# One pool of three PSUM banks for the prompt phase's row maxima, compressed outputs and transposes, in place of a pool of two and a pool of one

## The chip, the cores and the metric

The kernel runs on one core of a Trainium2 chip. The metric is the device time of one execution in microseconds (us). The core has a matrix engine (TensorE, PE in the profile, whose weight loads are listed as PEld), a vector engine (VectorE, DVE), a scalar engine (ScalarE, ACT), GpSimd (POOL) and SyncE (SP), which issues the transfers. Matrix results go to PSUM, which here is handed out as eight banks of 128 partitions by 512 fp32 values.

## The reference, cut to what matters

One decoder layer serves a prompt of 2048 tokens and a sample group of 32 tokens. Its attention branch, for 8 heads in 2 groups g of 4 heads r, looks at the keys in three ways and sums them with gates:

```python
sc = einsum('bgrtd,bngd->bgrtn', qg, kc) + bias        # compressed keys, 127 of them
pc = masked_softmax(sc, ...);  o_cmp = pc @ vc;  imp = pc @ cover
idx = top_k(score(imp), 8)                             # 8 blocks of 64 keys, per query
ps = masked_softmax(q @ k_selected + bias)             # selected branch "s"
pw = masked_softmax(q @ k_window + bias)               # window of 512 keys, branch "w"
o = g0 * o_cmp + g1 * (ps @ v_selected) + g2 * (pw @ v_window)
```

The rest of the layer is one input projection, a gated linear recurrence, two branch projections with gates, an output projection, a residual and a norm.

## The kernel before, in words

**Phases.** Up to about 1430 us of the span the kernel does the input projections beside the compression, the sample group's attention and the recurrence. Then comes the prompt phase (`prompt_phase`, line 1406), which the change touches. It walks 16 blocks of 128 queries in the order `ORDER` = 3, 2, 1, 0, 5, 4, 7, 6, ... , 12, 13 (line 1404); block number i stands for query tile t = ORDER[i].

**What a block needs.** Two blocks ahead, `prep` (line 1541) computes for each group g the compressed branch in five steps: `cmax` (the row maxima of the compressed scores, line 1550, reduced by DVE at 1552), `neg_row` (line 1416: two small DVE operations make `xd`, four PE products turn it into a row in PSUM, and ACT writes the row into the query operand, line 1426), `cs` (the scores, 1558 and 1559, and two exponentials on ACT), `cpv` (the compressed output, 12 products, read by a dozen small DVE operations that end in the choice of blocks `repp`, line 1579) and `sel` (a PE transpose, line 1584, and DVE writing the selection into the query operand, line 1585). One block ahead, `max_ops` (line 1488) computes row maxima of both branches: per chunk of up to 512 keys and head, products into a bank (lines 1518 and 1520) and one DVE reduction (line 1521); at the end `neg_row` again, whose row every final score product of that block (line 1643) needs. In the block itself, `score`, `probs` and `pv` make scores, exponentials and outputs, and `finish` (line 1656) transposes the block's sum (line 1660) and lets DVE multiply it (line 1672).

**Banks.** Eight are in use: two for `ps` (projections and, later, the merging products), two for `st` (scores), one for `po` (outputs), two in pool `pmx` (`mx`: every chunk of row maxima, `cmax`, `cpv`) and one in pool `ptr` (`tr`: `neg_row`, `sel`, `finish`). The code opens 608 tiles of `mx` and 128 of `tr` in the prompt phase. A tile is given a bank when its first product is scheduled, and the bank is free again after its last reader.

**Order of the work.** The order of each engine's queue is laid down when the kernel is built: the framework takes the instructions in program order, keeps a simulated time, and gives an engine the earliest instruction whose inputs and bank are ready by then. On the chip each engine goes through its queue in that order. Program order is made by hand in `run_block` (line 1883): list A holds the maxima of block i+1 and their `neg_row`, list B the `prep` steps of block i+2, both spread over the block's steps; `late` (line 1935) puts `finish` three steps behind its last output; `fill` (line 1850) puts in merging work (lines 1754 and 1786) of blocks that are done. Before the loop (lines 1607 to 1622) stand the `prep` of blocks 0 and 1 and the maxima of block 0. While the merging weights are not yet there, `fill` instead loads and splits them (`weights`, lines 1701 on ACT and 1702 on DVE), which in program order lies behind all that.

Of the kernel before, what the change touches and what calls it, by code (L numbers as in the profile page):

```python
# [10 lines left out]
F32 = mybir.dt.float32  # L11
# [7 lines left out]
PSUM = bass.MemoryType.PSUM  # L19
# [109 lines left out]
def trunk_kernel(ctx: ExitStack, tc: tile.TileContext, A, O):  # L129
# [1276 lines left out]
    def prompt_phase(a, st, pfill, state, sw):  # L1406
        KA, KB, V, TB, TQ = a["KA"], a["KB"], a["V"], a["TB"], a["TQ"]
        pu = st.enter_context(tc.tile_pool(name="pu", bufs=2, side="right"))
        pst = st.enter_context(tc.tile_pool(name="pst", bufs=2, space=PSUM, side="right"))
        ptr = st.enter_context(tc.tile_pool(name="ptr", bufs=1, space=PSUM, side="right"))  # L1410
        pmx = st.enter_context(tc.tile_pool(name="pmx", bufs=2, space=PSUM, side="right"))

        def flat(x):
            return x.rearrange("p r t -> p (r t)")

        def neg_row(m, dst):

            n = m.shape[2]
            x = pu.tile([128, 4, 4], F16, name="xd")[:, :, :2 * n]
            ve.tensor_scalar(x[:, :, :n], m, -1.0 / 1024, None, op0=OP.mult)  # L1420
            ve.scalar_tensor_tensor(x[:, :, n:], m, -1.0 / 1024, x[:, :, :n], op0=OP.mult, op1=OP.subtract)
            pt = ptr.tile([128, 4, 128], F32, name="tr")
            for r in range(4):
                mm(pt[:2 * n, r], x[:, r], a["id"], r == 0, True)

            ac.activation(dst, pt[:2 * n], AF.Identity, bias=a["nb"][:2 * n, n - 1:n], scale=1.0 / QS)

        def probs(ps, n, pool, bufs, sub):
            P = pool.tile([128, 512], F32, name="P", bufs=bufs[0])
            ph = pool.tile([128, 512], F16, name="Ph", bufs=bufs[1])  # L1430
            pl = pool.tile([128, 512], F16, name="Pl", bufs=bufs[1])
            ac.activation(P[:n], ps, AF.Exp, scale=1.0 / QS)  # L1432
            ac.activation(ph[:n], ps, AF.Exp, scale=1.0 / QS)  # L1433
            sub.tensor_sub(pl[:n], P[:n], ph[:n])  # L1434
            return ph, pl

        def pv(po, ph, pl, v, n, w, first, last):
            rs = [slice(r * 128, (r + 1) * 128) for r in range(4)]
            for r in range(4):
                mm(po[:, r, :w], ph[:n, rs[r]], v[:n, :w], first and r == 0, False)  # L1440
                mm(po[:, r, :64], ph[:n, rs[r]], v[:n, w:w + 64], False, False)  # L1441
            for r in range(4):
                mm(po[:, r, :w], pl[:n, rs[r]], v[:n, :w], False, last)  # L1443
# [44 lines left out]
        def max_ops(u, br, t, g):  # L1488
# [34 lines left out]
            def last():  # L1523
                ve.tensor_reduce(u["m"][:, :, "sw".index(br)], mp_[:, :, :nch], axis=AX.X, op=OP.max)
                if br == "s":
                    neg_row(u["m"], u["s"][96:100])
# [4 lines left out]
        def add_part(u, po, w):  # L1531

            new = "acc" not in u
            dst = pu.tile([128, 4, 64], F32, name="oacc", bufs=6) if new else pu.tile([128, 4, 64], F32, name="otmp", bufs=1)
            ve.tensor_tensor(dst, po[:, :, :64], w[:, :, None].to_broadcast([128, 4, 64]), op=OP.mult)  # L1535
            if new:
                u["acc"] = dst
            else:
                gp.tensor_add(u["acc"], u["acc"], dst)

        def prep(u, t, g):

            nv = 8 * t + 8
            nk = min(nv, 127)
            X = {}

            def cmax():
                pm = pmx.tile([128, 4, 128], F32, name="mx")
                for r in range(4):
                    mm(pm[:, r, :nv], u["c"][:96, r], u["k"][:96, :nv], r == 0, True)  # L1550
                m = pu.tile([128, 4], F32, name="mc")
                ve.tensor_reduce(m, pm[:, :, :nv], axis=AX.X, op=OP.max)
                ve.tensor_scalar(m, m, -10000.0 * QS, None, op0=OP.max)
                X["m"] = m

            def cs():
                ps = pst.tile([128, 512], F32, name="st")
                mm(ps[:nv], KB["c", g][:, :nv], flat(u["b"]), True, False)
                mm(ps[:nv], u["k"][:, :nv], flat(u["c"]), False, True)
                X["p"] = probs(ps[:nk], nk, pu, (1, 1), gp)  # L1560

            def cpv():
                po = pmx.tile([128, 4, 128], F32, name="mx")
                pv(po, *X["p"], V["c"][:, g], nk, 97, True, True)
                rs = po[:, :, 96]
                ve.tensor_scalar(rs, rs, TINY, None, op0=OP.max)
                ve.reciprocal(rs, rs)
                w = pu.tile([128, 4], F32, name="wc")
                ve.tensor_tensor(w, rs, gates[:, t, g * 4:g * 4 + 4], op=OP.mult)
                im = pu.tile([128, 32], F32, name="im")  # L1570

                for r in range(4):
                    ve.scalar_tensor_tensor(im, po[:, r, 64:96], rs[:, r:r + 1], im if r else a["sel0"][:, t], op0=OP.mult, op1=OP.add)
                add_part(u, po, w)
                m8 = pu.tile([128, 8], F32, name="m8p")
                ve.max(m8, im)
                rep = pu.tile([128, 32], F32, name="repp")
                ve.match_replace(rep, m8, im, -3e38)
                ve.tensor_tensor(rep, rep, im, op=OP.is_equal)
                X["rep"] = rep  # L1580

            def sel():
                pt = ptr.tile([128, 4, 128], F32, name="tr")
                pe.transpose(pt[:32, 0], X["rep"], ident)
                ve.tensor_scalar(u["s"][64:96], pt[:32, 0:1].to_broadcast([32, 4, 128]), -2.0 ** 15, None, op0=OP.mult)

            return [cmax, lambda: neg_row(X["m"][:, :, None], u["c"][96:98]), cs, cpv, sel]

        W_BUF = []
# [11 lines left out]
        def open_block(i):  # L1601
            units[i] = [loads(ORDER[i], g, i % 2) for g in range(2)]

        state["env"]["tp"] = lambda: ptr.tile([128, 4, 128], F32, name="tr").rearrange("p a b -> p (a b)")
        wc = sw.enter_context(tc.tile_pool(name="wc", bufs=3))
        state["env"]["piece"] = lambda: wc.tile([128, 512], F32, name="piece")
        for i in range(2):
# [16 lines left out]
        def main():  # L1624
# [29 lines left out]
            LA = {}  # L1654

            def finish(u, t, g, sz):
                pt = ptr.tile([128, 4, 128], F32, name="tr")
                ov = u["acc"].rearrange("p (a r) d -> p a (r d)", a=2)
                for k in range(2):
                    pe.transpose(pt[:, k], ov[:, k], ident)  # L1660
                q0 = t * 128
                rows = slice(g * 256, (g + 1) * 256)
                o = pp.tile([128, 2, 128], F32, name="oo", bufs=1)
                if t == ORDER[-1]:
                    if not LA:
                        for k in "hl":
                            LA["a" + k] = pu.tile([128, 512], F16, name="P" + k, bufs=1).rearrange("p (k t) -> p k t", k=4)
                    oh, ol = [LA["a" + k][:, 2 * g:2 * g + 2] for k in "hl"]
                else:
                    oh = pp.tile([128, 2, 128], F16, name="ooh", bufs=1)  # L1670
                    ol = pp.tile([128, 2, 128], F16, name="ool", bufs=1)
                ve.tensor_mul(o, pt[:, :2], sz)
                ac.activation(oh, o, AF.Copy)
                gp.tensor_sub(ol, o, oh)
                if t == ORDER[-1]:
                    return
                sy.dma_start(oah_d[rows, q0:q0 + 128].rearrange("(a p) t -> p a t", p=128), oh)
                sy.dma_start(oal_d[rows, q0:q0 + 128].rearrange("(a p) t -> p a t", p=128), ol)
# [204 lines left out]
            def run_block(i, t):  # L1883
# [24 lines left out]
                for x, (g, br, kt) in enumerate(tiles):  # L1908
# [14 lines left out]
                    if kt == t:  # L1923
                        epilogue(us[g], br, t, g, po)
                        if br == "s":
                            sz = pp.tile([128, 2, 128], F32, name="szt")
                            sy.dma_start(sz, sz_d[g * 256:(g + 1) * 256, t * 128:t * 128 + 128].rearrange("(a p) t -> p a t", p=128))

                            def fin(g=g, sz=sz):
                                finish(us[g], t, g, sz)  # L1930
                                if g == 1:
                                    done.add(t)
                                    fs["hold"] = max(fs["hold"], R["now"] + 4)

                            late.append((R["now"] + 3, fin))
# [22 lines left out]
    with ExitStack() as s2:  # L1958
        sw, sb = ExitStack(), ExitStack()
        load_x, fill, state = make_projections(s2, sw, sb)  # L1960
# [57 lines left out]
```

## Time and profile before

| what | value |
|---|---|
| median of 3 runs | 2497.49 us (2493.37 to 2504.09) |
| profiled execution | 2498.46 us, span of the core 2496.1 us |
| mean granted TensorE clock | 0.974 of full |
| PE busy | 2357.9 us (94% of the span) |
| DVE, ACT, POOL busy | 1575.8, 1198.0, 989.9 us |

The span is the time from the first to the last instruction of the core; the execution's own time has some 2 us around it. Busy times of different engines overlap, and an idle engine costs time only where others wait for it. A line "PE mx L1518 <- DVE mpw L1521" among the waits says that PE, at the product of line 1518 that writes a tile `mx`, sat idle until the DVE instruction of line 1521 that writes `mpw` was done: since that one reads the bank that PE wants to write, it is a wait for a bank.

### The profile page before, as it was taken

The page shows a single profiled execution, that of the slowest core. Times are in us where ns is not written, and L with a number is a line of the kernel's source. Part 1 is how long each engine was busy: PE and PEld are TensorE (multiplying, and loading weights), DVE is VectorE, ACT ScalarE, POOL GpSimd, SP SyncE. Part 2 cuts the span into 40 slices and gives each one's busy share as a digit, 9 for nine tenths or more (in the row PEclk, how much of TensorE's full clock was granted, in tenths as well). Part 3 has the DMA queues.
Part 4 walks back from the last instruction along what each step waited for, and adds up shares of the span by engine and source line. Part 5 has one row for each costly group of instructions (what it writes and reads, how often), then busy time and mean ns, then how long its engine had stood idle before and what let it go on. Part 6 is the DMA issues. An engine that isn't in the chain of part 4 may idle for free.

```text
span 2496.1 us, 57172 instructions
## 1 busy us (share of the span) xinstructions
PE 2357.9 (94%) x22228; PEld 1554.0 (62%) x22228; DVE 1575.8 (63%) x4232; ACT 1198.0 (48%) x2639; POOL 989.9 (40%) x1179
## 2 busy tenths in 40 slices
PE   5999999998999999999989969899999999999998
PEld 4988675554785555555555446656666666565765
DVE  7556455656325688777763667677777767767543
ACT  5544333422223366555552346436555666667763
POOL 0100102332102255444550006536656666677864
PEclk9999999999999999999999979999999999999999
DMA  6543314656322434333323652322222221211121
GB/s 202 170 121 115 121 69 163 218 205 217 131 65 105 144 105 132 115 118 97 109 87 98 192 159 63 79 81 69 78 58 72 57 66 51 63 52 45 48 59 46
DMA packets 266719, 264.96 MB, mean 106 GB/s; under 512 B 95100, under 2 KB 237872, under 8 KB 259280
## 3 DMA queue, kind: packets, MB, share of 16 engines
q1 hardware_dynamic: 257936, 223.56, 29.0%
q0 software_dynamic: 8512, 37.75, 4.6%
q8 instruction: 175, 2.87, 0.5%
q14 instruction: 96, 0.79, 0.1%
HBM read 181.84 MB, written 83.55 MB: 106 GB/s over the span
## 4 chain that ended last, share of the span: by engine, by line
PE 68%; DVE 14%; DMA 7%; ACT 4%; issue 4%; POOL 1%; SPq 1%; DVEq 0%; ACTq 0%; POOLq 0%
PE ps L361 14%; PE ps L440 9%; PE ps L1786 7%; PE ps L1754 6%; PE ps L421 4%; PE st L1643 3%; PE st L1633 3%; PE mx L1518 3%; DVE X L683 2%; DMA wraw<-in_w_in_dram 2%; PE ph L920 2%; PE po L1440 2%; PE po L1443 2%; PE po L1441 2%; DVE mps L1521 1%
## 5 line engine op out<-in xcount | busy, mean ns | idle before, releaser
L1434 POOL TENSOR_TENSOR Pl<-P,Ph 128x512 f16<-128x512 f32 (+5 forms) x444 | 516.6, 1173 | 406.8 <-ACT Ph L1433 171.6
L1432 ACT ACTIVATE P<-st 128x512 f32<-128x512 f32 (+3 forms) x444 | 264.6, 596 | 204.8 <-PE st L1643 157.5
L361 PEld LDWEIGHTS <-wh 128*128 128x128 f16 x2240 | 214.3, 99 | 190.4 <-issue 45.2
L1433 ACT ACTIVATE Ph<-st 128x512 f16<-128x512 f32 (+5 forms) x444 | 262.6, 593 | 14.9 <-PE po L1441 10.8
L361 PE MATMUL ps<-xh,wh 128*128 128x512 f16 (+1 forms) x1120 | 234.5, 344 | 11.0 <-DVE row L374 5.1
L1521 DVE TENSOR_REDUCE mps<-mx 128x1 f32<-128x512 f32 (+3 forms) x320 | 189.2, 605 | 75.9 <-PE mx L1518 45.7
L361 PE MATMUL ps<-xl,wh 128*128 128x512 f16 (+1 forms) x1120 | 236.0, 347 | 1.1 <-issue 1.0
L361 PE MATMUL ps<-xh,wl 128*128 128x512 f16 (+1 forms) x1120 | 232.3, 341 | 0.0
L440 PE MATMUL ps<-wh,xh 128*128 128x256 f16 (+3 forms) x680 | 189.4, 279 | 7.0 <-ACT to L447 4.3
L440 PE MATMUL ps<-wh,xl 128*128 128x256 f16 (+3 forms) x680 | 188.4, 278 | 4.0 <-DVE xl L327 4.0
L440 PE MATMUL ps<-wl,xh 128*128 128x256 f16 (+3 forms) x680 | 189.0, 278 | 0.0
L1440 PEld LDWEIGHTS <-Ph 128*128 128x128 f16 (+5 forms) x1776 | 138.8, 98 | 41.3 <-issue 6.9
L361 PEld LDWEIGHTS <-wl 128*128 128x128 f16 x1120 | 107.9, 98 | 86.3 <-issue 9.4
L1441 PEld LDWEIGHTS <-Ph 128*128 128x128 f16 (+5 forms) x1776 | 128.7, 96 | 32.7 <-issue 1.4
L440 PEld LDWEIGHTS <-xh 128*128 128x128 f16 (+1 forms) x1360 | 129.9, 99 | 30.7 <-issue 6.5
L686 POOL TENSOR_TENSOR X<-X,kt 128x128 f32<-128x128 f32 x160 | 81.8, 512 | 142.8 <-ACT X L685 142.8
L1521 DVE TENSOR_REDUCE mpw<-mx 128x1 f32<-128x512 f32 (+3 forms) x224 | 104.9, 485 | 49.6 <-PE mx L1520 46.7
L652 POOL TENSOR_TENSOR Xo<-Xo,qt 128x256 f32<-128x256 f32 x32 | 30.5, 953 | 260.4 <-ACT Xo L651 229.3
L1754 PEld LDWEIGHTS <-xh 128*128 128x128 f16 x1280 | 105.3, 98 | 30.3 <-issue 9.1
L1518 PE MATMUL mx<-kas,qs 96*128 96x512 f16 (+3 forms) x320 | 109.8, 355 | 10.4 <-DVE mps L1521 7.7
L1443 PEld LDWEIGHTS <-Pl 128*128 128x128 f16 (+3 forms) x1776 | 96.1, 97 | 30.9 <-POOL Pl L1434 8.4
L1440 PE MATMUL po<-vs,Ph 128*128 128x65 f16 x1088 | 106.6, 192 | 0.8 <-DVE otmp L1535 0.8
(538 smaller groups left out, 5918.9 us busy)
## 6 DMA issues: line engine op xcount, KB each, us to landing
wraw<-in_w_in_dram SPq DMA_DIRECT2D x22, 1024.0 KB
xt<-in_x_prompt_dram SPq DMA_DIRECT2D x32, 512.0 KB
ma_d<-row SPq DMA_DIRECT2D x8, 1040.0 KB
out_y_prompt_dram<-xt SPq DMA_DIRECT2D x16, 512.0 KB
sg<-ma_d SPq DMA_DIRECT2D x56, 128.0 KB
sg<-mb_d SPq DMA_DIRECT2D x56, 128.0 KB
mb_d<-row SPq DMA_DIRECT2D x18, 256.0 KB
q_d<-row SPq DMA_DIRECT2D x4, 1040.0 KB
```

Source lines behind the costliest of these rows:

```text
L361: mm(ps, l[:, kc], xs(r, t0, n)[:, kc], k == 0, k == 23)
L440: mm(ps, xs(l, t0, r)[:, kc], w[:, kc], k == 0, k == 23)
L1432: ac.activation(P[:n], ps, AF.Exp, scale=1.0 / QS)
L1433: ac.activation(ph[:n], ps, AF.Exp, scale=1.0 / QS)
L1434: sub.tensor_sub(pl[:n], P[:n], ph[:n])
L1440: mm(po[:, r, :w], ph[:n, rs[r]], v[:n, :w], first and r == 0, False)
L1441: mm(po[:, r, :64], ph[:n, rs[r]], v[:n, w:w + 64], False, False)
L1443: mm(po[:, r, :w], pl[:n, rs[r]], v[:n, :w], False, last)
L1518: mm(pmf[:, (x - ka) * 128:(y - ka) * 128], qq[:K, r], kk, i == 0, not sp_)
L1521: ve.tensor_reduce(mp_[:, r, c:c + 1], pmf[:, :n], axis=AX.X, op=OP.max)
L1754: mm(X["ps"], w[:, kc, cs], os_[o][:, kc], k == 0, k == 11)
L1786: mm(X["ps"], X["y"][y][:, kc, i0:i0 + r], W["o", kc // 4][w][:, kc % 4, cs], k == 0, k == 23)
```

## The change

The pool `ptr` is gone, `pmx` has three banks in place of two, and the tiles that were `tr` are taken from it under the name `mx`. All 736 tiles of the prompt phase now come from one pool. The number of banks in use stays eight. The last use that the diff touches (`env["tp"]`, for scaling projection weights) has no instruction left in the prompt phase: the last such load was at 1347.8 us.

```diff
-        ptr = st.enter_context(tc.tile_pool(name="ptr", bufs=1, space=PSUM, side="right"))
-        pmx = st.enter_context(tc.tile_pool(name="pmx", bufs=2, space=PSUM, side="right"))
+        pmx = st.enter_context(tc.tile_pool(name="pmx", bufs=3, space=PSUM, side="right"))
...
         def neg_row(m, dst):
-            pt = ptr.tile([128, 4, 128], F32, name="tr")
+            pt = pmx.tile([128, 4, 128], F32, name="mx")
...
             def sel():
-                pt = ptr.tile([128, 4, 128], F32, name="tr")
+                pt = pmx.tile([128, 4, 128], F32, name="mx")
...
-        state["env"]["tp"] = lambda: ptr.tile([128, 4, 128], F32, name="tr").rearrange("p a b -> p (a b)")
+        state["env"]["tp"] = lambda: pmx.tile([128, 4, 128], F32, name="mx").rearrange("p a b -> p (a b)")
...
             def finish(u, t, g, sz):
-                pt = ptr.tile([128, 4, 128], F32, name="tr")
+                pt = pmx.tile([128, 4, 128], F32, name="mx")
```

## Rows read from the trace of the kernel before

**Rows 1.** The page: busy times, and two of its 40-slice lines.

```profile
PE 2357.9 (94%) x22228; PEld 1554.0 (62%) x22228; DVE 1575.8 (63%) x4232; ACT 1198.0 (48%) x2639; POOL 989.9 (40%) x1179
...
PE   5999999998999999999989969899999999999998
...
PEclk9999999999999999999999979999999999999999
```

**Rows 2.** Windows: length; busy of PE, PEld, DVE, ACT, POOL; PEclk, DMA, GB/s.

```profile
1460.00:1503.00 43.00, 21.86 (x172) 12.66 (x171) 34.79 (x83) 18.94 (x27) 2.79 (x4) 0.53 0.53 157
...
1540.00:1600.00 60.00, 51.91 (x583) 33.08 (x582) 38.03 (x166) 32.76 (x63) 37.55 (x38) 1.00 0.25 63
1600.00:2400.00 800.00, 782.21 (x8646) 522.65 (x8645) 560.07 (x1498) 472.04 (x919) 509.63 (x493) 0.98 0.22 62
2400.00:2496.10 96.10, 84.89 (x1048) 57.31 (x1045) 38.04 (x121) 46.18 (x100) 51.99 (x57) 0.97 0.18 56
```

**Rows 3.** PE's waits from 1455 to 1503 us: total, times, longest.

```profile
PE mx L1518 <- DVE mpw L1521: 6.8, 5, 1.8
PE tr L1424 <- DVE qs L1585: 3.7, 1, 3.7
...
PE mx L1518 <- DVE mps L1521: 2.6, 2, 2.4
...
PE tr L1424 <- ACT qc L1426: 0.8, 1, 0.8
```

**Rows 4.** PE in order of time, 1450 to 1505 us: start, length, instruction.

```profile
1450.74 0.21 PE L1440 MATMUL mx<-vc,Ph 32*128 32x97 f16 x1
...
1452.58 0.25 PE L1550 MATMUL mx<-kac,qc 96*128 96x24 f16 x4
...
1459.89 0.27 PE L1584 MATMUL tr<-ident,repp 128*32 128x128 f32 x1 [0.78 <-DVE mc L1553]
...
1464.57 0.58 PE L1424 MATMUL tr<-h_id,xd 128*2 128x128 f16 x4 [3.72 <-DVE qs L1585]
...
1471.52 0.26 PE L1440 MATMUL mx<-vc,Ph 24*128 24x97 f16 x1 [0.61 <-ACT Ph L1433]
...
1474.81 0.61 PE L1518 MATMUL mx<-kw,qs 96*128 96x256 f16 x2 [1.52 <-DVE oacc L1535]
...
1488.65 0.42 PE L1584 MATMUL tr<-ident,repp 128*32 128x128 f32 x1
...
1502.17 1.01 PE L1643 MATMUL st<-qs,kw 100*128 100x512 f16 x2
```

**Rows 5.** DVE in order of time, 1460 to 1465 us.

```profile
1460.09 0.17 DVE L1421 SCALAR_TENSOR_TENSOR xd<-mc,xd 128x4 f16<-128x4 f32 x1
1461.11 2.70 DVE L1702 SCALAR_TENSOR_TENSOR xl<-wraw,swb,xh 128x1024 f16<-128x1024 f32 x2 [0.85 <-ACT xh L1701]
```

**Rows 6.** DVE's groups from 1460 to 1503 us: busy, mean ns, idle before.

```profile
L1702 DVE SCALAR_TENSOR_TENSOR xl<-wraw,swo,xh 128x1024 f16<-128x1024 f32 x8 | 10.3, 1282 | 3.8 <-ACT xh L1701 3.8
L1521 DVE TENSOR_REDUCE mps<-mx 128x1 f32<-128x512 f32 x8 | 5.4, 689 | 1.2 <-PE mx L1520 1.0
```

**Rows 7.** PE's waits from 1503 to 2400 us: total, times, longest.

```profile
PE mx L1518 <- DVE mps L1521: 5.8, 16, 1.0
...
PE mx L1518 <- DVE mpw L1521: 1.9, 5, 0.7
```

**Rows 8.** PE in order of time, between two blocks and near the end.

```profile
2021.54 0.59 PE L1550 MATMUL mx<-kac,qc 96*128 96x128 f16 x4
...
2026.64 0.58 PE L1424 MATMUL tr<-h_id,xd 128*4 128x128 f16 x4
...
2368.34 0.38 PE L1660 MATMUL tr<-ident,oacc 128*128 128x128 f32 x2
...
2370.12 0.38 PE L1518 MATMUL mx<-kas,qs 96*128 96x512 f16 x1
```

**Rows 9.** The window around that passage between two blocks, columns as in rows 2.

```profile
2015.00:2030.00 15.00, 12.43 (x98) 7.93 (x97) 13.17 (x31) 4.08 (x8) 4.24 (x4) 0.66 0.26 83
```

## The prediction

> **What bounds the kernel now.** I read the page first: PE is busy for 94% of the span, and nearly every slice of its line says 9 [rows 1]. So what any change of banks can give back is time in which PE idles or runs slowly. The clock line has one dip, just where the prompt phase begins. Windows over that phase [rows 2] then show where PE's time is lost: from 1460 to 1503 us PE is busy for 21.9 of 43 us, at a granted clock of 0.53, so mostly at the lower of its two levels (1.2 instead of 2.4 GHz); from 1540 to 1600 us it idles for 8.1 us; in the 800 us after that for 17.8 us in all. The last 96 us hold no maxima and are out of the change's reach. What PE waits for there is the third view. In the first stretch [rows 3] the largest wait is for a bank of maxima (6.8 us for branch "w", 2.6 us for "s", together 9.4), and next the single bank of transposes (3.7 and 0.8 us). In the 897 us from 1503 on, the waits for banks of maxima are small: 5.8 and 1.9 us [rows 7], 7.7 in all.
>
> One property of the pools has to be read from the order of time. If the 736 tiles are numbered in program order and set against the starts in the trace, no `mx` tile starts before an earlier `mx` tile, and no `tr` tile before an earlier `tr` tile. Across the two pools 180 tiles do start before an earlier one of the other pool. The first is the `cmax` of block 1 at 1452.58 us, which program order has behind the `sel` of block 0 that runs at 1459.89 [rows 4]; the last is a `finish` at 2368.34 us, which stands behind the maximum that starts at 2370.12 [rows 8]. So a pool hands out its banks in program order, and after the change these 180 can no longer overtake.
>
> **The change, part by part.** No instruction is added or removed: the same products, reductions and transposes run, no DMA moves to another place in the program, and no engine is given other work. What changes is which bank a product waits for, and with that the order in which the queues are laid.
>
> *The single transpose bank at the start.* The `neg_row` of block 1 has its `xd` complete by 1460.26 us (1460.09 + 0.17) [rows 5], but its products start at 1464.57, after 3.72 us of waiting for DVE line 1585 [rows 4]. That one empties the transpose bank; DVE spent 2.70 us on two weight splits in between [rows 5]. The second `neg_row` waits another 0.8 us for the first one's reader [rows 3]. With three banks neither waits: 4.5 us. They lie on a chain, since behind them stand the compressed scores, the compressed outputs of block 1 (the second at 1471.52 us) and only then the first row maximum, at 1474.81 [rows 4]. So the outputs come at about 1467.0.
>
> *The order of one pool at the start.* Against this, the maxima of block 0 now stand behind the `sel` of block 1, of which the second runs at 1488.65 us today, 13.8 us behind the first maximum [rows 4]. How long it takes when nothing overtakes it the trace doesn't show. The nearest rows are those of block 0, where the second compressed output starts at 1450.74 and the second `sel` at 1459.89: 9.15 us. From 1467.0 that gives 1476.2, so the maxima start 1.4 us later than now. Bounds: 4.5 us earlier if the `sel` is no hindrance, some 13.8 later if its place stays. I take +1.4, since the rows of block 0 are the same instructions.
>
> *The third bank for the maxima of block 0.* From 1474.81 us 16 maxima pass, 8 reductions for each branch, at 0.69 us [rows 6] 11.0 us of DVE; PE waited 9.4 us for their banks [rows 3]. In those gaps DVE took weight splits of 1.28 us, 10.3 us of them in the window [rows 6]. These lie behind the maxima in program order: with a third product ready the maximum goes first and the split waits. Upper bound 9.4 us; lower bound 0, since DVE is busy for 34.8 of the 43 us anyway [rows 2] and the splits must run at some time. What is late next is then the merging work of the sample tokens, which needs the weights, and it has slack. I take −8: near the upper bound, because the work in the gaps can wait.
>
> *From 1503 us on.* The 7.7 us of waits [rows 7] go at most. Against that stand passages between blocks. At 2021.54 us the `cmax` of a coming block starts before the `neg_row` of the next block, which runs at 2026.64 [rows 8]; it and the tiles behind it may not do so after the change, and PE has less to fill that passage with. There are 15 such passages, and 49 of the 180 overtaking tiles passed a `neg_row` of this kind; at 0.6 us a tile (the `cmax` took 0.59) [rows 8] that is 29 us of PE work, the bound if PE had nothing else and the row came no sooner. But the same tiles' reductions keep DVE from the row today, and merging work is mostly there. Bounds: −7.7 and +29 less 7.7, so +21. I take −5, nearer to the waits than to the 29 us, since the passage's own chain gets shorter as its filling goes.
>
> *Sum.* +1.4 − 8 − 5 = −11.6 us (the 4.5 us are inside the +1.4). The profiled execution took 2498.46 us, 1 us above the median of the runs, so the same step from the median 2497.49 gives 2485.9; I say **2486**.
>
> A difference under 0.5%, 12.5 us here, is about what a measurement of this kernel can't tell from none (its runs lie 2493.37 to 2504.09). The forecast is just inside that.
>
> **The rivals.**
>
> *The weights keep DVE.* DVE is the bound in the start stretch, and the third bank only lets products wait in PSUM rather than before it. For it: 34.8 of 43 us [rows 2]. Against it: the splits come later in program order. Then the second term is 0 and the rest gives 1.4 − 5 = −3.6: 2494 us.
>
> *All bank waits go.* 4.5 + 9.4 [rows 3] + 7.7 [rows 7] = 21.6 us, if the order of one pool costs nothing: 2476 us. For it: PE is the bound, and each of these waits is PE's own. Against it: the 180 tiles. The Trainium skill, on its page "Perfetto Trace Analysis", section "Optimizing Tensor Performance", has independent groups of products rotate through different banks so that emptying one overlaps the next; by this rule alone this rival would be the forecast.
>
> *The queue of one pool blocks (slower).* The place is the passage between blocks: one `neg_row` that waits for its DVE chain now holds up every later maximum and `cmax`. If half of the 29 us is not covered, and the gains at the start are eaten by the `sel`, the time is 2497.5 + 14.5 + 1.4 = 2513 us. It decides from the point at which the uncovered part is more than the 13 us of gains (8 + 5), some 0.9 us in each of 15 passages. For it: the 180 tiles. Against it: PE idles only 17.8 of 800 us now [rows 2], so there is other work.
>
> *The clock falls more often.* From 2015 to 2030 us PE was busy for 12.4 of 15 us and was granted 0.66 [rows 9], where the 800 us around it have 0.98 [rows 2]. Waits that gather in such passages could bring this to more of them: 0.34 of 15 us is 5 us for each, so four more of them without other gain give 2498 + 20 − 7 = 2511. The Trainium skill, on its page "TensorE: Matmul & The Clock Gate", section "A second HAM failure mode: psum-queue depth-cycling", tells of a kernel whose passing through PSUM banks left many small gaps, between which the clock fell and rose. The clock in these rows agrees so far; that more cycling brings more of it no row here shows.
>
> *The change doesn't do what it says.* A `tr` tile may hold the third bank whenever a maximum could use it, and the pool works as two and one did: about 2497.
>
> **How the numbers follow.** The forecast with its own spread (2478 to 2491) has 0.50, of which 0.30 lies beyond 12.5 us of gain, by the bounds of its second and third terms. The weights rival has 0.18 and the idle third bank 0.06, nearly all within 0.5%. All waits gone has 0.09, all of it faster. The blocking queue has 0.12 and the clock 0.05, both slower but for a weak form. Together: faster 0.39, same 0.45, slower 0.16. The range reaches from 2470, beyond the rival in which all waits go, to 2508, short of the two slower ones: 0.04 and some 0.14 are left out.
>
> **What would show it.** Right: from 1460 to about 1490 us PE's waits for line 1521 nearly gone, no wait of `neg_row` for line 1585, weight splits on DVE bunched behind the maxima, and the first final score product (line 1643) near 1495 us instead of at 1502 [rows 4]; the stretch at the lower clock shorter by about as much; from 1503 on PE idle for some 5 us less. Wrong: the second `sel` of block 1 still near 1488 with the maxima behind it; or PE's idle time between blocks up by 1 us or more each, with waits on `xd` or on the ACT of line 1426; or more windows with a granted clock under 0.9 between 1600 and 2400 us. If PE's idle time in the prompt phase stays at today's value and the time moves all the same, the order of the queues has changed something that I have not priced.

## The result, and the profile after

The median of six runs is 2478.36 us (2469.68 to 2480.13) against 2494.36 us of the kernel before (six runs, 2491.56 to 2504.09): a ratio of 0.9922, 95% interval 0.9906 to 0.9937. The profiled executions took 2478.31 and 2498.46 us, with spans of 2476.5 and 2496.1 us. The one of before is some 4 us above its median, so of the 19.6 us between the spans about 16 are the change's.

The instructions are the same; the deletion of a line moves the lines of the changed region up by one (1521 is now 1520, and so on), and what was written `tr` is now `mx`. The page of the kernel after:

```profile
PE 2340.4 (95%) x22228; PEld 1548.1 (63%) x22228; DVE 1574.7 (64%) x4232; ACT 1196.7 (48%) x2639; POOL 991.2 (40%) x1179
```

Windows of the kernel after, to be held against [rows 2] (columns as there):

```profile
1460.00:1503.00 43.00, 21.25 (x190) 12.72 (x191) 34.61 (x89) 18.29 (x29) 4.04 (x5) 0.56 0.53 158
1503.00:1540.00 37.00, 35.09 (x486) 22.04 (x482) 27.97 (x94) 22.34 (x47) 23.64 (x27) 1.00 0.26 64
1540.00:1600.00 60.00, 53.57 (x579) 33.31 (x579) 40.27 (x165) 32.25 (x63) 36.61 (x37) 0.97 0.24 60
1600.00:2400.00 800.00, 783.89 (x8851) 526.64 (x8850) 570.17 (x1536) 479.19 (x941) 521.05 (x501) 1.00 0.22 64
```

and one window of the kernel before that [rows 2] leave out:

```profile
1503.00:1540.00 37.00, 36.21 (x510) 23.31 (x509) 30.96 (x96) 23.80 (x50) 23.99 (x27) 0.99 0.27 71
```

PE's idle time has hardly moved: 16.1 us in the 800 us from 1600 on (17.8 before), 6.4 in 1540 to 1600 (8.1 before), 21.8 in the start stretch (21.1 before). What has moved is the clock: 1.00 where it was 0.98, and 8851 products in the 800 us where there were 8646. Taken in pieces of 50 us, the kernel before has four in which the granted clock fell below 1.00:

```profile
1650.00:1700.00 50.00, 47.66 (x519) 32.48 (x518) 34.85 (x111) 28.36 (x55) 29.44 (x30) 0.93 0.31 89
...
1850.00:1900.00 50.00, 47.47 (x440) 27.99 (x438) 37.62 (x110) 22.93 (x47) 22.26 (x22) 0.93 0.21 63
...
2000.00:2050.00 50.00, 46.97 (x529) 31.68 (x526) 37.66 (x110) 30.82 (x59) 34.15 (x33) 0.90 0.22 62
...
2150.00:2200.00 50.00, 47.83 (x558) 33.35 (x559) 34.50 (x91) 29.69 (x56) 33.80 (x34) 0.93 0.16 41
```

and the kernel after has one:

```profile
1650.00:1700.00 50.00, 46.01 (x538) 32.05 (x536) 37.30 (x118) 30.11 (x59) 31.62 (x31) 0.97 0.27 77
```

The clock missing from full, times 50 us, is (0.07 + 0.07 + 0.10 + 0.07) x 50 = 15.5 us before and 1.5 us after: 14.0 us. Two windows ahead of these change it a little: from 1540 to 1600 us the clock is 0.97 after and was 1.00 before (1.8 us lost), and from 1503 to 1540 us it is 1.00 and was 0.99 (0.4 us won). That leaves 12.6 us. The first final score product starts at 1499.77 us (1502.17 before) [rows 4], so 2.4 us were won up to there and 17.2 behind it. Of the 17.2 the clock is up to 12.6 (an upper value, since PE idles for part of the low stretches), PE's idle time is 1.7 + 1.7 - 1.1 = 2.3 us (1540 to 1600, from 1600, 1503 to 1540), and some 2 us are in neither.

A second trace of the kernel after, from its repetition at the end of the experiments (span 2478.8 us), shows which part repeats:

```profile
1502.10 0.77 PE L1642 MATMUL st<-qs,kw 100*128 100x512 f16 x2
```

```profile
1600.00:2400.00 800.00, 783.31 (x8828) 526.26 (x8827) 570.21 (x1532) 477.65 (x938) 519.57 (x500) 1.00 0.23 64
```

Behind the first final score it has 976.7 us, as the first trace has (976.7, against 993.9 before), and the clock is again at 1.00. But its first final score is as late as that of the kernel before. So the gain lies behind the start. Over the runs the clock's part is smaller than in the two profiles: on the chip of the repetition the mean granted clock is 0.9775 over six runs of the kernel after and 0.9745 over eleven of the kernel before; 1 less these, times the mean times (2482.9 and 2501.2 us), is 56 and 64 us of missing clock, so some 8 of 18 us.

**The start.** PE in order of time in the kernel after:

```profile
1432.59 0.25 PE L1549 MATMUL mx<-kac,qc 96*128 96x32 f16 x4 [0.89 <-DMA qb<-qh_d]
...
1455.82 0.27 PE L1583 MATMUL mx<-ident,repp 128*32 128x128 f32 x1
1455.93 0.35 PE L1549 MATMUL mx<-kac,qc 96*128 96x24 f16 x8
1462.75 0.66 PE L1423 MATMUL mx<-h_id,xd 128*2 128x128 f16 x8 [4.84 <-DVE xd L1420]
...
1469.90 0.26 PE L1439 MATMUL mx<-vc,Ph 24*128 24x97 f16 x1 [0.59 <-ACT Ph L1432]
...
1479.12 0.37 PE L1583 MATMUL mx<-ident,repp 128*32 128x128 f32 x1 [6.53 <-DVE repp L1578]
1479.29 0.63 PE L1517 MATMUL mx<-kw,qs 96*128 96x256 f16 x2
...
1499.77 1.06 PE L1642 MATMUL st<-qs,kw 100*128 100x512 f16 x2
```

The first row is the `cmax` of block 0. In the kernel before it is this:

```profile
1433.79 0.26 PE L1550 MATMUL mx<-kac,qc 96*128 96x32 f16 x4
```

From it to the first final score are 68.4 us before, 67.2 after, and 69.0 in the second trace (from 1433.05 us). So half of the 2.4 us was there before the prompt phase began, and the rest doesn't repeat.

The first `cmax` of block 1 no longer overtakes the second `sel` of block 0: it waits until 1455.93, and its `neg_row` then waits 4.84 us for its input where it waited 3.72 us for its bank [rows 4]. Both of the pair go at once (x8 products). The second `sel` of block 1 runs at 1479.12 instead of 1488.65, and the maxima stand behind it. So the order of one pool is what the prediction had read from the 180 overtaking tiles; matched the same way, the kernel after has none. PE's waits from 1455 to 1503 us:

```profile
PE mx L1583 <- DVE repp L1578: 6.5, 1, 6.5
PE mx L1423 <- DVE xd L1420: 4.8, 1, 4.8
...
PE mx L1517 <- DVE mpw L1520: 2.9, 3, 1.5
...
PE mx L1517 <- DVE mps L1520: 1.3, 1, 1.3
```

Waits for banks of maxima are down from 9.4 to 4.2 us [rows 3], and waits at the head of the one queue have taken their place. The view of the kernel before has one more wait of line 1518 for a bank, which [rows 3] leave out, and which the kernel after doesn't have:

```profile
PE mx L1518 <- DVE oacc L1535: 2.7, 2, 1.5
```

Here the bank is held by a compressed output, whose last reader is line 1535. The second output of block 1 starts at 1471.52 us [rows 4], and DVE comes to that reader more than 10 us later:

```profile
1481.93 0.42 DVE L1535 TENSOR_TENSOR oacc<-mx,wc 128x256 f32<-128x256 f32 x1
```

**A passage between two blocks.** Between block 9 and block 10 the kernel before does this (PE in order of time; the first row is block 9's last final score product, the last block 10's first):

```profile
2014.12 0.38 PE L1643 MATMUL st<-qs,kas 100*128 100x512 f16 x1
...
2017.28 0.38 PE L1518 MATMUL mx<-kas,qs 96*128 96x512 f16 x1 [0.31 <-DVE mps L1521]
...
2019.31 0.58 PE L1518 MATMUL mx<-kas,qs 96*128 96x512 f16 x1 [0.51 <-DVE mps L1521]
...
2020.88 0.58 PE L1518 MATMUL mx<-kas,qs 96*128 96x512 f16 x1 [0.16 <-DVE mps L1521]
...
2024.75 0.59 PE L1424 MATMUL tr<-h_id,xd 128*4 128x128 f16 x4
...
2027.15 1.03 PE L1643 MATMUL st<-qs,kw 100*128 100x512 f16 x2
```

and the kernel after this:

```profile
2005.27 0.38 PE L1642 MATMUL st<-qs,kas 100*128 100x512 f16 x1
...
2008.20 0.39 PE L1423 MATMUL mx<-h_id,xd 128*4 128x128 f16 x4 [1.38 <-DVE xd L1420]
2008.77 0.39 PE L1423 MATMUL mx<-h_id,xd 128*4 128x128 f16 x4
...
2009.76 0.60 PE L1642 MATMUL st<-qs,kw 100*128 100x512 f16 x2
```

Before, when block 9 has no score left to do, five maxima of block 10 are still outstanding, among them ones that wait for a bank; 13.0 us pass until the next final score. From 2019.31 us on a product of the same shape takes 0.58 us instead of 0.38: the clock has fallen. After, no maximum is outstanding, the two `neg_row` start 0.57 us apart (1.89 before: 2024.75 and 2026.64 [rows 8]), and 4.5 us pass. The windows of these two passages, before and after:

```profile
2014.10:2027.20 13.10, 10.53 (x90) 6.60 (x89) 12.48 (x28) 1.76 (x3) 4.31 (x4) 0.69 0.32 100
```

```profile
2004.90:2009.80 4.90, 3.52 (x56) 2.27 (x55) 4.83 (x13) 2.66 (x5) 2.71 (x3) 1.00 0.18 41
```

DVE is busy nearly throughout in both; the passage is the DVE chain that was not done in time. Counted over the last 11 passages (from block 4 on), 28 maxima of the coming block start behind a block's last final score product before and 4 after, and these passages add up to 80.3 and 51.4 us. Such maxima are called late below. The 28.9 us between the two sums are not all loss: in the passage shown, the kernel before also does five maxima of block 11, which the kernel after does behind it (90 products in the window against 56).

### The profile page after: what moved, and what is told of

It is laid out like the page before. It is cut to its first block, busy times and chain, and to the rows that moved or that the text cites. A ratio compares the mean times of both kernels' runs of the same rounds, so it can differ in the third digit from the quotient of the medians.

```text
span 2476.5 us, 57155 instructions
## 1 busy us (share of the span) xinstructions
PE 2340.4 (95%) x22228; PEld 1548.1 (63%) x22228; DVE 1574.7 (64%) x4232; ACT 1196.7 (48%) x2639; POOL 991.2 (40%) x1179
## 4 chain that ended last, share of the span: by engine, by line
PE 68%; DVE 13%; DMA 7%; issue 5%; ACT 4%; POOL 2%; SPq 1%; DVEq 0%; POOLq 0%; ACTq 0%
PE ps L361 14%; PE ps L440 9%; PE ps L1785 7%; PE ps L1753 7%; PE ps L421 4%; PE mx L1517 3%; PE st L1632 3%; PE st L1642 3%; DVE X L683 2%; PE ph L920 2%; PE po L1439 2%; PE po L1442 2%; PE po L1440 2%; DMA wraw<-in_w_in_dram 2%; PE pt L903 1%
## 5 line engine op out<-in xcount | busy, mean ns | idle before, releaser
L1433 POOL TENSOR_TENSOR Pl<-P,Ph 128x512 f16<-128x512 f32 (+3 forms) x444 | 516.0, 1173 | 380.0 <-ACT Ph L1432 274.9
L1432 ACT ACTIVATE Ph<-st 128x512 f16<-128x512 f32 (+3 forms) x444 | 262.3, 594 | 11.1 <-PE po L1440 8.7
L1439 PEld LDWEIGHTS <-Ph 128*128 128x128 f16 (+4 forms) x1776 | 138.8, 98 | 43.6 <-issue 6.2
L1440 PEld LDWEIGHTS <-Ph 128*128 128x128 f16 (+4 forms) x1776 | 128.8, 96 | 34.5 <-issue 2.8
L1517 PE MATMUL mx<-kas,qs 96*128 96x512 f16 (+3 forms) x320 | 103.7, 353 | 6.1 <-DVE mps L1520 2.3
```

The lines of the kernel that those rows point to most:

```text
L1517: mm(pmf[:, (x - ka) * 128:(y - ka) * 128], qq[:K, r], kk, i == 0, not sp_)
```

## The experiments

The time of an experiment stands beside runs of the kernel before on the same chips; since those differ a little from chip to chip, the ratio is what is compared.

**Theories at the outset.** A: the pair of `neg_row` no longer passes one bank. B: row maxima and compressed outputs find more banks. C: maxima and `cmax` can no longer overtake `neg_row` and fill DVE in front of it.

### Only neg_row in the pool of two

```diff
-            pt = ptr.tile([128, 4, 128], F32, name="tr")
+            pt = pmx.tile([128, 4, 128], F32, name="mx")
```

> Kernel before, but neg_row alone takes its bank from the pool of two; sel and finish keep their own bank. Theory A (the second neg_row of a pair no longer waits for the first one's reader, so the passages between blocks shorten and the clock holds there): most of the 16 us, about 2482 us, with the pair's starts under 0.5 us apart and fewer low-clock stretches after 1600 us. Theory B (row maxima gain from a third bank): no third bank here, so 2494 or slower. Theory C (what counts is that maxima and cmax of the coming block can no longer overtake neg_row): as A, about 2482.

2522.13 us, ratio 1.0088 (1.0057 to 1.012): slower. 41 maxima are late in the 11 passages. PE's waits from 1503 to 2400 us:

```profile
PE mx L1518 <- DVE mps L1521: 10.0, 21, 1.2
...
PE mx L1518 <- DVE mpw L1521: 2.1, 4, 0.8
```

Against 7.7 us [rows 7], 12.1 us of waits for banks of maxima. B stands. A and C get no gain here, but the run takes room from the maxima at the same time, so it doesn't try them alone; the third and fourth experiment do.

### Only sel and finish in the pool of two

```diff
-                pt = ptr.tile([128, 4, 128], F32, name="tr")
+                pt = pmx.tile([128, 4, 128], F32, name="mx")
```

> Kernel before, but sel and finish take their bank from the pool of two; neg_row keeps the single bank for itself. Theory A: the pair of neg_row still passes one bank, so about 2494 (at most 3 us less, since nothing else holds that bank). Theory B: sel and finish take banks from the maxima, so slower, 2496 to 2502. Theory C: maxima may still overtake neg_row, so about 2494.

2518.03 us, ratio 1.0066 (1.0043 to 1.0088), 40 maxima late. So it matters little which transposes crowd the pool of two, and the loss is larger than B had expected.

### The pair of neg_row in one tile

```diff
+                if br == "s" and g == 0:
+                    PAIR.append(u)
+                elif br == "s":
+                    us = [PAIR.pop(), u]
+                    pt = ptr.tile([128, 4, 128], F32, name="tr")
+                    for j, v in enumerate(us):
...
+                            mm(pt[32 * j:32 * j + 4, r], x[:, r], a["id"], r == 0, True)
+                    for j, v in enumerate(us):
+                        ac.activation(v["s"][96:100], pt[32 * j:32 * j + 4], AF.Identity, bias=a["nb"][32 * j:32 * j + 4, 1:2], scale=1.0 / QS)
```

> Kernel before with its three banks and both pools, but the two neg_rows at the end of a block's maxima share one tile (partitions 0 to 3 and 32 to 35), products first and both readers after. Maxima may still overtake. Theory A: most of the gain, about 2482, pair starts close together. Theory B: no gain, 2494. Theory C: no gain, 2492 to 2496.

2505.35 us, ratio 1.0009 (0.9994 to 1.0025): no gain, and 28 late as before. The edit has a cost of its own, since the first row of a pair now waits for the second one's `xd`, and the 11 passages add up to 91.0 us. But in the kernel before there is little to win: from 1503 to 2400 us its `neg_row` waits 1.4 us in all for the single bank, 0.4 us behind a `sel` and the rest behind a `finish`:

```profile
PE tr L1424 <- DVE oo L1672: 1.0, 2, 0.6
```

Together these leave next to nothing of A: the pair's closeness in the kernel after is there, but it buys no 16 us.

### No overtaking, with the banks of before

The products of a maximum and of `cmax` are issued behind the last product of the latest `neg_row` in program order (`behind()` is `tc.issue_after(NEG[-1])`).

```diff
+            if n == 2:
+                NEG.append(y.ins)
...
+                with behind():
                     for i, (x, y, kk) in enumerate(runs):
                         mm(pmf[:, (x - ka) * 128:(y - ka) * 128], qq[:K, r], kk, i == 0, not sp_)
```

> Kernel before with its banks and pools, and one added rule: products of maxima and cmax that stand behind a neg_row of a block's maxima in program order stay behind it in PE's queue. The pair still passes one bank. Theory A: no gain, 2494, or slower since PE loses filling, up to 2500. Theory B: no gain, 2494. Theory C: most of the gain, about 2482, with the first neg_row of a pair earlier after the last maximum.

2514.76 us, ratio 1.005 (1.0028 to 1.0072). The order that the one pool brings costs time when it comes alone. The window from 1600 to 2400 us of this kernel:

```profile
1600.00:2400.00 800.00, 769.11 (x8565) 516.97 (x8563) 566.10 (x1506) 465.50 (x905) 504.81 (x486) 0.98 0.22 61
```

PE idles for 30.9 us where nothing overtakes, 13 us more than before [rows 2]: the work that passed a waiting `neg_row` did fill PE. The 11 passages are even shorter than before (75.0 us, with 36 maxima late), so their length alone doesn't set the time. C falls.

### One pool of two banks

```diff
-        pmx = st.enter_context(tc.tile_pool(name="pmx", bufs=3, space=PSUM, side="right"))
+        pmx = st.enter_context(tc.tile_pool(name="pmx", bufs=2, space=PSUM, side="right"))
```

> Kernel after with two banks in its one pool, the third left empty. Theory B: the maxima find fewer banks than in the kernel before, more of them late than its 28, and the time is above that of the runs in which only some transposes moved into a pool of two (2518 and 2522): 2525 to 2550. Theory D (sharing itself helps): near 2494 or under it.

This is the kernel after with one bank less. 2544.38 us, ratio 1.0176 (1.0159 to 1.0193); 52 maxima late. PE's waits from 1503 to 2400 us:

```profile
PE mx L1517 <- DVE mps L1520: 11.2, 26, 1.0
...
PE mx L1517 <- DVE mpw L1520: 5.3, 8, 2.1
PE mx L1517 <- DVE oacc L1534: 3.4, 3, 2.5
```

In the kernel after, the same view has 1.0 for `mps`, 2.1 for `mpw` and nothing for `oacc`, the reader of a compressed output. As to time, the third bank of the one pool is worth 1.0176 - 0.9922 = 2.5%: two banks for all are 1.8% slower than two and one kept apart, and three for all 0.8% faster. B holds; D, that sharing helps whatever the number of banks, falls.

### Three banks for the maxima alone

The second replacement stands at all four places that took a `tr`.

```diff
-        pmx = st.enter_context(tc.tile_pool(name="pmx", bufs=2, space=PSUM, side="right"))
+        pmx = st.enter_context(tc.tile_pool(name="pmx", bufs=3, space=PSUM, side="right"))
-                pt = ptr.tile([128, 4, 128], F32, name="tr")
+                pt = state["fps"].tile([128, 512], F32, name="ps").rearrange("p (a b) -> p a b", a=4)
```

> Kernel before, but the pool of mx has three banks for itself, and the transposes (neg_row, sel, finish) have none of their own: they take turns with the merging products in the pool of ps. Theory B, as it now stands (what counts is how many banks the row maxima and compressed outputs find: with more, the maxima of the coming block are not behind when a block's scores end): the passages between blocks get short, few maxima late (before: 28 over the last 11 passages, after: 4), and about 2480 us, unless transposes that wait behind merging products eat it. Theory D (it is the sharing with transposes, not the number of banks): no gain, 2494 or slower.

2516.72 us, ratio 1.0065 (1.0047 to 1.0083), a loss, but with no maximum late from block 4 on. A row from the start of its prompt phase, and a late window:

```profile
1429.71 0.27 PE L1549 MATMUL mx<-kac,qc 96*128 96x32 f16 x4 [32.94 <-DMA qc<-tc_d]
```

```profile
1630.00:2400.00 770.00, 755.96 (x8605) 509.73 (x8604) 536.47 (x1446) 455.93 (x900) 496.05 (x482) 1.00 0.23 66
```

From 1630 us to 2400 it runs as the kernel after does, at 1.00 and with PE idle for 14.0 of 770 us (16.1 after, 17.0 before). It loses ahead of that. PE stands for 32.9 us in front of the first `cmax`, where the kernel before has its projections to do (PE busy for 24.9 of the 30 us from 1400 to 1430, here 0.3), and from 1503 to 1630 us PE idles for 17.5 of 127 us, at 0.93 (9.7 before, at 1.00). The projections take their bank from `ps`, as the transposes now do, and go on only behind the two `neg_row` of block 0. This fits a pool that hands out its banks in program order, as in the prediction's reading of the pools; that it is the cause is argued, since no run takes it apart. As a test of B by time it is inconclusive; in the late stretch it speaks for B.

### The compressed outputs on the transposes' bank

```diff
             def cpv():
-                po = pmx.tile([128, 4, 128], F32, name="mx")
+                po = ptr.tile([128, 4, 128], F32, name="tr")
```

> Kernel before with one edit: the compressed outputs (cpv) take the single bank of the transposes, and the pool of two serves row maxima and cmax alone. Theory B, with the compressed outputs as the tiles that hold a bank long: maxima find both banks more often, fewer than 28 late, about 2485 us, less what transposes lose behind the outputs. If the long-held outputs are not the hindrance: 2494 or slower, with as many late as before.

2491.52 us, ratio 0.9954 (0.9939 to 0.997): with the banks and pools of before, moving 32 of 608 tiles to the other pool brings more than half of the gain. A compressed output is read from its bank by eight DVE operations (lines 1566 to 1573 and 1535), a maximum by one. Matched tile by tile in the kernel before, from 1503 us on, an output has its bank for 4.4 us on the mean, from its first product to the end of its last reader, and a maximum for 1.3 us. In a pool of two, a pair of outputs leaves no bank. But its profiled execution (2498.54 us, span 2496.6) is the slowest of its runs, which go down to 2485.72, and has 25 late maxima, so how the gain comes about can't be read from it. By the clock it is not: the mean granted clock of its five runs is 0.9744, that of the eight of before beside them 0.9749. So it is not shown that the kernel after gains in this way.

### The maxima earlier in the block, with the banks of before

```diff
-                    while ai < len(A) and ai < (x + 1) * len(A) / (n * 0.95):
+                    while ai < len(A) and ai < (x + 1) * len(A) / (n * 0.80):
```

> Kernel before with its banks and pools; only the hand-made pacing differs: list A (the row maxima of the coming block) is spread over 0.80 of a block's steps instead of 0.95. Theory B' (lateness of the maxima at the end of a block is what costs, and banks are one way to it): fewer than the 28 late maxima over the last 11 passages, and 2483 to 2490 us. If it is the number of banks and not lateness, or if the two banks hold the maxima back whatever the pacing: 28 late or more, 2494 us or slower.

2517.23 us, ratio 1.0064 (1.0046 to 1.0082), though with 20 late instead of 28 the passages shorten to 57.1 us. So B' holds in the count of late maxima and fails in the time: they are a sign and not the cost. PE's waits from 1503 to 2400 us:

```profile
PE mx L1518 <- DVE mps L1521: 9.0, 18, 1.1
PE st L1633 <- ACT Ph L1433: 7.9, 22, 0.7
...
PE mx L1518 <- DVE mpw L1521: 1.7, 3, 0.8
```

Asked for more in less time, two banks make PE wait inside the blocks: 10.7 us of bank waits instead of 7.7 [rows 7], and 7.9 us of waits for a bank of the scores instead of 3.3. The clock falls too: 0.9705 on the mean of four runs against 0.9745 of the eleven of before, which is some 10 of the 15 us lost. In order of the waits of line 1518 (`mps` and `mpw` in this window; the kernels built on the kernel after, below, are left out) stand after 3.1, compressed outputs moved 6.9, before 7.7, pair in one tile 8.3, no overtaking 9.4, `sel` and `finish` in the pool of two 9.7, this 10.7, `neg_row` there 12.1, one pool of two 16.5 us. The ratios are 0.992, 0.995, 1, 1.001, 1.005, 1.007, 1.006, 1.009 and 1.018, in the same order but for one pair that the intervals don't part. The exception is three banks for the maxima alone (8.3 us, 1.0065), which loses at the start. The waits differ by 13 us and the times by some 64, so they go along with the loss and are not the whole of it.

### On top of the kernel after

```diff
+            for k, p in enumerate(zip(*c)):         # before the loop over blocks
+                if (i, k) == (1, 4):
+                    later = p                       # the two sel of block 1
+                    continue
...
+        for x in later:                             # behind the maxima of block 0
+            x()
```

> Kernel after, with the two sel of block 1 put behind the row maxima of block 0 in program order, before the loop over blocks. If the wait of 6.5 us for repp in front of the first maximum (1472 to 1479 us) is on the path that sets the end, the first maximum comes some 5 us earlier and the time is 2472 to 2475 (ratio to before about 0.990). If DVE bounds that stretch whatever the order, as before and after have the same DVE work in it, no change from after: 2478, ratio 0.992.

> The kernel after once more, beside the next three on the same chip, as their yardstick: ratio to before 0.991 to 0.994.

> Kernel after with the two sel of block 1 behind the row maxima of block 0, measured again beside the kernel after. If the order at the start is worth something: a ratio to before lower by 0.001 to 0.003 than that of the kernel after. If DVE bounds the start whatever the order: the same ratio as the kernel after.

The kernel after, once more: 2482.15 us, ratio 0.9925 (0.991 to 0.994). With `sel` moved: 2475.94 us, ratio 0.9892 (0.987 to 0.9913), and beside the kernel after 2478.75 us, ratio 0.9901 (0.9886 to 0.9917). Both times the ratio is lower by 0.002 to 0.003. The intervals of the ratios overlap, but on the one chip all five runs with `sel` moved (2475.05 to 2479.88) lie under all six of the kernel after (2480.68 to 2487.14). So the order at the start is worth 3 to 5 us (by the medians and by the means). The start itself is shorter, 64.3 us from the `cmax` of block 0 to the first final score (64.2 in the first run) where the kernel after has 67.2 and 69.0:

```profile
1435.33 0.25 PE L1549 MATMUL mx<-kac,qc 96*128 96x32 f16 x4
...
1499.66 1.06 PE L1647 MATMUL st<-qs,kw 100*128 100x512 f16 x2
```

The 6.5 us for `repp` are gone from the start, and PE's waits there (1455 to 1503 us, second run) now read:

```profile
PE mx L1423 <- DVE xd L1420: 11.0, 2, 5.8
PE mx L1517 <- DVE mpw L1520: 7.4, 5, 2.3
```

The wait has moved again, with DVE's work in the window the same (34.0 of 43 us), but the scores come earlier: that DVE bounds the start whatever the order doesn't hold. The pacing of 0.80 on top of that:

> Kernel after, with the two sel of block 1 moved and with the pacing of 0.80. Only 4 to 6 maxima are late without the pacing, so by theory B' little is left: the same as the run without it, within 4 us. If the passages' DVE chain behind the last maximum is what is left of their length: 2 to 8 us faster.

2478.07 us, ratio 0.9898 (0.9881 to 0.9915), with no maximum late and the passages down to 32.4 us: no difference from the run without it. Where the maxima have banks, they may come early without loss, but nothing is left to win by it.

## Why the prediction was right or wrong

**Direction and size.** 2486 us was forecast, and 2478.4 measured, 0.8% under before and inside the range; the forecast stood just inside "no difference", and the gain is beyond 0.5%. The sum was -11.6 us against some -16. That it is so near is in part luck: the two terms of the start, -6.6 us together, came to nothing that repeats, and the term of -5 for the rest came to most of the gain, by a way that it had not priced.

**The single transpose bank and the order of one pool at the start (+1.4).** The sign was right and the size was not: the maxima start at 1479.3 us, 4.5 later than before, where 1476.2 was forecast. The second half went as worked out: from the second compressed output to the second `sel` it is 9.2 us (1469.90 to 1479.12), and 9.15 was taken from block 0. The first half didn't: the outputs come 1.6 us earlier and not 4.5. The wait of `neg_row` for its bank did go, but it became a wait for `xd`, since `cmax` now stands behind `sel`. That was the price of order that the step had put only on the maxima.

**The third bank for the maxima of block 0 (-8).** This step failed in what it took for free. From the first maximum to the first final score it is 20.5 us instead of 27.4, so the stretch did shrink, by 6.9. But it shrank because the `sel` of block 1 and the readers of its outputs now run in front of it, and hardly because the weight splits wait: four of them start in it (1479.4 to 1490.4 us), where six did before. With the later start the final scores came 2.4 us earlier in the one trace, and counted from the `cmax` of block 0 they are 1.2 us earlier there and 0.7 later in the second. The step was also worked out without the 2.7 us behind a compressed output, which stood in the same view. As to time, the rival "the weights keep DVE" came nearer: DVE was busy for 34.6 of the 43 us as before (34.8). But the run with `sel` moved, with the same work on DVE, reaches its scores 3 to 5 us sooner, so the order in the queues holds the start too.

**From 1503 us on (-5).** A shorter chain in the passages is there, as the step had it, but its size was off by about a factor of three: 17.2 us between the profiles, of which some 4 are that the profile of before is above its median. PE's idle time, which the step was made of, fell by 2.3 us. The waits that it counted fell from 7.7 to 3.1, and others came in their place. Most of the rest, up to 12.6 us in the two profiles and some 8 us over the runs, is clock, which the step had put at nothing. The row for it was on the table: 0.66 in the passage [rows 9]. It was used only for the rival in which the clock falls more often. The prediction had named this outcome among its signs: idle time as before and the time moved all the same means that something was not priced.

**The blocking queue, and the clock.** The order of one pool does cost what this rival feared: +0.5% when it comes alone (no overtaking), and 6.9 us of waits for `xd` from 1503 us on in the kernel after:

```profile
PE mx L1423 <- DVE xd L1420: 6.9, 8, 1.5
...
PE mx L1517 <- DVE mpw L1520: 2.1, 3, 0.9
...
PE mx L1517 <- DVE mps L1520: 1.0, 3, 0.6
```

But with a third bank there are 4 late maxima, and the DVE chain in front of `neg_row` is short. The rival's bound of 29 us was priced with a `cmax` of 0.59 us, a row at the low clock; at the full clock of the kernel after the same four products take 0.39 us. And matched tile by tile, 59 and not 49 of the 180 pass a `neg_row` of blocks 1 to 15. The other rival, in which the clock falls more often, went the other way: with more banks in the pool 1.5 us of clock are missing from 1600 to 2400 us where there had been 15.5. The Trainium skill's page "TensorE: Matmul & The Clock Gate", section "A second HAM failure mode: psum-queue depth-cycling", tells of gaps that came with the cycling through banks, and says nothing of how many banks there are. In this case the clock was low in a passage with gaps (0.69, with PE busy for 10.5 of 13.1 us), which agrees so far; with more banks it was low for less time.

**All bank waits go.** The number (2476) is near the result; the way is not. Waits for banks behind the maxima's own readers fell from 17.1 to 7.3 us in the two views (9.4 + 7.7, 4.2 + 3.1), other waits came in their place, and PE idles about as long as before. The rule of the Trainium skill that stood beside it ("Perfetto Trace Analysis", section "Optimizing Tensor Performance") agrees with the outcome of the one pool, where a third bank to rotate through is worth 2.5%.

**What is shown and what stays open.** Shown: neither the pair's single bank nor the order of one pool brings the gain; a bank less in the one pool costs 2.5%; taking the compressed outputs away from the maxima brings 0.5% with no bank added; and the gain lies behind the first final score, in two traces of the kernel after against one of the kernel before, with fewer bank waits, fewer late maxima and fewer stretches at the low clock. Open: how the 0.8% divides between the outputs' long hold and the room for maxima at large; why the gain of the outputs alone comes without clock; where the part of the gain lies that is neither clock nor idle time; and whether the clock falls in a passage because of its gaps or of the sparse products in it. No run sets the clock apart from the gaps, so that the clock is a cause of the gain, and not only its share in the sum, is not shown.

## What to carry to other kernels

Before banks are counted, look at how long each kind of tile holds one. Here 32 tiles with eight readers each held theirs more than three times as long as a row maximum; another pool for them brought 0.5%, and a third bank in the one pool 2.5%, with 7.7 us of bank waits in view. A pool that hands out banks in program order turns a merger into a queue, so number the tiles and see which overtake today; that order cost 0.5% here when it came without a bank. And where PE is the bound, look at the clock of the stretch around a gap as well as at the gap: here 15.5 us of clock were missing from 1600 to 2400 us, beside 17.8 us of idle time.

## What was not expected

The runs of one kernel can differ by their clock. Of the kernel after, the fastest (2469.68 us) had a mean granted clock of 0.981 and the slowest (2480.13 us) 0.977; 0.004 of 2476 us is 9.9 us, and the times differ by 10.5. It is not the only thing by which runs differ: of the last kernel above, with `sel` moved and the pacing of 0.80, the fastest run (2473.67 us) had 0.976 and the slowest (2479.84 us) 0.979. So a single profile of these kernels can be 10 us off, and this is as large as most terms of the sum. It is also why one pair of profiles puts two thirds of the gain on the clock, and the runs of one chip less than half.
